# An identity made in DRAM, S5 input matrices loaded in rows and turned by TensorE, and small rows on other queues

## The chip, the cores and the metric

The kernel runs on one NeuronCore of a Trainium2 chip. A core has five engines that run their own instruction streams and meet through semaphores: TensorE (PE, with its weight loads as PEld), VectorE (DVE), ScalarE (ACT), GpSimd (POOL) and SyncE (SP). SP does no arithmetic here; it issues transfers. ACT and POOL issue a few transfers too, each on a queue of its own. The metric is the device time of one execution in microseconds (us), as the median of repeated runs.

## The reference

One layer of a diffusion backbone over 256 latent tokens, with 256 context tokens, all in float32, width 1024:

```python
mod = silu(c) @ w_mod + b_mod                  # shift, scale, gate; the same from c_ctx for the context
h   = rmsnorm(x, norm1_g) * (1 + sc1) + sh1    # and hc from ctx
proj = h @ w_in                                # columns: S5 input | K | V | Q | branch gates
# branch A: bidirectional S5, 32 groups of 16 channels, 64 complex states per group and direction
lbar = exp(lam * exp(log_step));  bbar = ((lbar - 1) / lam)[..., None] * (b_re + 1j * b_im)
#   diagonal scan over the context, its last state into the scan over the latents, readout with c, gelu, GLU
# branch B: grouped-query attention, normalised q and k, rotary positions
x_mix = x + g1 * (gates_a * (s @ w_ssm_out) + gates_b * (o @ w_attn_out)) @ w_out
# top 4 of 32 SwiGLU experts on the normalised x_mix: w_gate_up (1024 x 2048), w_down (1024 x 1024) each
out = rmsnorm(x_mix + g2 * experts, final_norm_g)
```

The S5 input matrices `s5_b_re` and `s5_b_im` have the shape direction x group x state x channel, 2 x 32 x 64 x 16 numbers each.

## The kernel before

On-chip memory is 24 pages of 128 partitions x 2048 numbers, and nearly everything lives in them. A transfer into a page may start only when the last reader of its earlier content is through. SP issues the large transfers strictly in program order (`load`, line 103). Behind the front part a list of 1 MB weight pieces (`stream`) is fed through pages as they come free (`release`): gates, GLU, output projections, and then per expert eight pieces of w_gate_up and four of w_down. The instructions of TensorE, VectorE and ScalarE come from a scheduler in the opening part, and from line 711 on mostly in the order in which they are written.

The opening part, to which all of the change belongs, goes so:

- SP loads x and ctx (four transfers of 512 KB), the small rows of the S5 eigenvalues (`lrows`, `lst`), then the modulation weights. `load_mod0(c, kk, page)` brings two 512 KB pieces of w_mod; c = 0 and c = 1 are two halves of the columns, four calls each. The two 1 MB pieces of the S5 input projection (`wu`) come between, and so do the four transfers of `s5_b_re` and `s5_b_im` into `b_raw` (lines 231 to 233). Those put the state index on the partitions, so that each run that is contiguous in DRAM is 16 numbers, 64 bytes.
- The identity matrix `ident`, by which TensorE transposes, is made on POOL by a fill and a masked select (`make_identity`, line 246; it shows as masks.py lines 197 and 199). The counting ramp `iot` (line 254) and the triangle `tri` are made there too.
- ScalarE and VectorE take the mean squares of x and ctx (`ss`); VectorE makes the reciprocal root from them (`rsqrt` into `rs`), by which both scale x and ctx in place.
- TensorE transposes the small rows `rows` into columns `cols`; from them come `sig` and the modulation input `scond`. It transposes `lrows` into `lam`, from which VectorE works out the S5 constants (`exp_acc` first).
- `h_raw` transposes x and ctx (32 transposes, copied out by ScalarE and VectorE into `hT`), while `mod0_mm(0, kk)` multiplies `scond` by the first half of the modulation weights. `mod0_copy`, `mod0_T` and `mod0_rows` turn the result into per-channel scale and shift, which are put on `hT`. Then `u_mm` (the S5 input projection) runs in turn with `mod0_mm(1, k)`.
- VectorE meanwhile makes `BB`, the scaled input matrices, from `b_raw`, and then, after `mod0_rows(1)`, the tables of `v_tables`.

Of the kernel before, what the change touches and what calls it, by code (L numbers as in the profile page):

```python
# [11 lines left out]
F32 = mybir.dt.float32  # L12
# [21 lines left out]
def hybrid_block(ctx: ExitStack, tc: tile.TileContext, a: dict, out: bass.AP):  # L34
    nc = tc.nc
# [20 lines left out]
    def w(name, *idx):  # L56
        return a[name][(0,) + idx] if idx else a[name][0]
# [16 lines left out]
    def sm(shape, name, dt=F32):  # L74
        return pool.tile(shape, dt, name=name)
# [27 lines left out]
    def load(dst, src):  # L103
        return tc.keep_in_program_order(SP.dma_start(dst, src))  # L104
# [11 lines left out]
    rows = sm([48, 128], "rows")  # L116
# [5 lines left out]
    load(lrows[0:32], w("s5_lam_re").rearrange("d g n -> g d n"))  # L122
    load(lrows[32:64], w("s5_lam_im").rearrange("d g n -> g d n"))
    load(lst[64:96], w("s5_log_step").rearrange("d g -> g d"))
    S.dma_start(rows[0:8], a["c"].rearrange("b (k p) -> (b k) p", p=128))
    S.dma_start(rows[8:16], a["c_ctx"].rearrange("(k p) -> k p", p=128))
    S.dma_start(rows[16:24], a["norm1_g"].rearrange("b (k p) -> (b k) p", p=128))
    G.dma_start(rows[28:44], w("b_mod")[0:2048].rearrange("(k p) -> k p", p=128))
    G.dma_start(rows[24:28], a["b_glu"].rearrange("b (k p) -> (b k) p", p=128))
# [97 lines left out]
    wu = [load_cols(w_in, 0, 512, 22, 0, 4)]  # L227
    for kk in range(4):
        load_mod0(1, kk, (18, 19, 20, 11)[kk])
        if kk == 0:  # L230
            for r, nm in ((0, "s5_b_re"), (1, "s5_b_im")):
                for d in range(2):
                    load(b_raw[64 * d:64 * d + 64, r], w(nm, d).rearrange("g n p -> n g p"))
        if kk == 2:
            wu.append(load_cols(w_in, 0, 512, 21, 4, 4))
# [9 lines left out]
    ident = sm([128, 128], "ident")  # L245
    make_identity(nc, ident)
# [97 lines left out]
    G.tensor_copy(lrows[64:96], lst[64:96].unsqueeze(2).to_broadcast([32, 2, 64]))  # L344
    ttrans(pl[:, 0:96], lrows.rearrange("p d n -> p (d n)"), ident[0:96, 0:96])
    lam = sm([128, 3, 32], "lam")
    with tc.issue_after(last.ins):
        V.tensor_copy(lam.rearrange("p r g -> p (r g)"), pl[:, 0:96])
# [203 lines left out]


# [1237 lines left out]
```

## Time and profile before

| | |
|---|---|
| runs, median (lowest to highest) | 1270.48 us (1269.86 to 1271.14) |
| the profiled execution | 1271.41 us |
| its span, first to last instruction | 1269.6 us |
| busy: PE / DVE / ACT / POOL | 1164.9 / 395.5 / 191.9 / 41.8 us |
| moved by the DMA engines | 462.54 MB, 364 GB/s over the span |
| DMA packets, and those under 512 B | 119134, 20669 |

The profile is of one execution. Its time is 1.8 us longer than its span; what lies around the span is launch and end. The span is read in stretches: an opening until about 92 us, the S5, attention and projection part until about 340 us, and the 32 experts after it.

### The profile page before, as it was taken

To read this page: it belongs to the slowest core of one execution; us is meant where nothing else is said; L and a number is where in the kernel's file an instruction comes from. 1 tells how busy PE (TensorE), PEld (TensorE's weight loads), DVE (VectorE), ACT (ScalarE), POOL (GpSimd) and SP (SyncE) were. 2 spreads that over 40 slices of the span, in tenths; PEclk is the share of its full clock that TensorE was granted. 3 is DMA by queue.
4 is the path that set the end of the run, shared out by engine and by line. 5 is a ranking of instruction groups with operands and counts; after the bars stand their busy time and mean duration, and the time that the engine had idled before them with its cause. 6 is when DMAs were issued, how large, how long until landed. Compare 5 with 4: busy or idle time off the path is not lost.

```text
span 1269.6 us, 16157 instructions
## 1 busy us (share of the span) xinstructions
PE 1164.9 (92%) x6759; PEld 532.9 (42%) x6760; DVE 395.5 (31%) x869; ACT 191.9 (15%) x358; POOL 41.8 (3%) x69
## 2 busy tenths in 40 slices
PE   3999996899899999999999898989898989999886
PEld 2775675798333333333323232323232323333224
DVE  4999963574211211111212111111111111111111
ACT  3241384542100000000000000000000000000002
POOL 1100140020000000000000000000000000000000
PEclk9999997999899999999999999999999999999999
DMA  9957484888899999999999999999999999999996
GB/s 283 303 194 263 139 194 98 278 317 333 331 412 417 416 417 417 416 417 417 417 417 417 418 416 418 417 418 416 417 418 417 417 416 417 417 416 417 416 392 196
DMA packets 119134, 462.54 MB, mean 364 GB/s; under 512 B 20669, under 2 KB 42345, under 8 KB 84242
## 3 DMA queue, kind: packets, MB, share of 16 engines
q1 hardware_dynamic: 117570, 458.31, 91.8%
q0 software_dynamic: 1440, 3.15, 1.4%
q8 instruction: 55, 0.90, 0.3%
q14 instruction: 21, 0.17, 0.0%
q10 hardware_dynamic: 48, 0.01, 0.0%
HBM read 459.89 MB, written 1.54 MB: 363 GB/s over the span
## 4 chain that ended last, share of the span: by engine, by line
PE 57%; DMA 32%; DVE 6%; issue 2%; ACT 2%; SPq 1%; POOL 0%; DVEq 0%; ACTq 0%; POOLq 0%
PE bk L97 54%; DMA pg<-in_w_gate_up_dram 28%; DVE pg L49 5%; PE bk L100 2%; DMA pg<-in_w_down_dram 2%; DMA pg<-in_b_gate_up_dram 2%; ACT pg L49 1%; SPq L104 1%; DMA pg<-in_w_in_dram 0%; DVE LS L49 0%; DVE smx L49 0%; ACT L49 0%; DVE rs_t L49 0%; DVE gate L49 0%; DVE gs__2634 L49 0%
## 5 line engine op out<-in xcount | busy, mean ns | idle before, releaser
L97 PE MATMUL bk<-pg,pg 128*64 128x512 f32 (+6 forms) x5424 | 998.7, 470 | 55.0 <-DMA pg<-in_w_down_dram 28.5
L97 PEld LDWEIGHTS bk<-pg,pg 128*64 128x64 f32 (+3 forms) x5424 | 445.0, 150 | 548.6 <-issue 360.4
L49 ACT ACTIVATE pg<-bk 128x512 f32<-128x512 f32 (+4 forms) x154 | 76.2, 521 | 745.1 <-PE bk L100 677.6
L49 DVE TENSOR_SCALAR pg<-bk 128x512 f32<-128x512 f32 x64 | 44.3, 692 | 294.3 <-PE bk L97 294.3
L49 DVE TENSOR_TENSOR pg<-pg,pg 128x1024 f32<-128x1024 f32 (+9 forms) x136 | 117.8, 891 | 25.6 <-ACT pg L49 24.4
L49 ACT ACTIVATE pg<-pg 128x512 f32<-128x512 f32 (+9 forms) x112 | 76.6, 697 | 246.9 <-DVE pg L49 214.9
L49 DVE TENSOR_TENSOR pg<-bk,shT 128x512 f32<-128x512 f32 x32 | 22.1, 692 | 270.5 <-PE bk L97 270.5
L49 DVE TENSOR_TENSOR pg<-bk,pg 128x512 f32<-128x512 f32 (+4 forms) x52 | 32.2, 619 | 221.2 <-PE bk L97 219.4
L100 PE MATMUL bk<-ident,pg 128*128 128x128 f32 x448 | 72.8, 290 | 10.6 <-DVE cmx L49 6.1
L100 PEld LDWEIGHTS bk<-ident,pg 128*128 128x128 f32 x448 | 50.6, 145 | 71.8 <-issue 42.0
L97 PE MATMUL bk<-pg 64*128 64x512 f32 (+1 forms) x368 | 70.3, 483 | 0.0
L97 PEld LDWEIGHTS bk<-pg 64*128 64x128 f32 (+1 forms) x368 | 19.8, 159 | 50.1 <-issue 50.1
L49 DVE TENSOR_TENSOR pg<-pg 128x512 f32<-128x512 f32 (+3 forms) x89 | 37.3, 434 | 3.6 <-ACT pg L49 3.0
L97 PE MATMUL bk<-pg,selB 128*64 128x512 bf16 (+1 forms) x196 | 34.3, 388 | 0.0
L49 DVE SCALAR_TENSOR_TENSOR pg<-pg 128x512 f32<-128x512 f32 (+3 forms) x67 | 30.3, 459 | 10.1 <-DMA pg<-in_x_dram 4.6
L1645 POOL DMA_DIRECT2D pg<-g2d x2 | 1.3, 640 | 887.3 <-PE bk L97 887.3
L97 PE MATMUL bk<-pg,scond 128*32 128x256 f32 (+1 forms) x256 | 26.9, 518 | 0.0
L49 DVE TENSOR_SCALAR pg<-iot,posp,gate 128x128 f32<-128x128 f32 x64 | 18.9, 340 | 0.0
L49 DVE TENSOR_TENSOR pg<-pg,LS 128x64 f32<-128x64 f32 (+4 forms) x36 | 15.9, 470 | 0.2
L97 PEld LDWEIGHTS <-selB 128*64 128x64 bf16 x196 | 9.0, 108 | 16.1 <-issue 15.9
L49 DVE TENSOR_SCALAR pg<-iot,posp,rs 128x64 f32<-128x64 f32 x64 | 15.7, 308 | 0.1
L49 DVE COPY pg<-bk 128x512 f32<-128x512 f32 (+1 forms) x24 | 14.5, 613 | 2.5 <-PE bk L100 2.5
(148 smaller groups left out, 180.1 us busy)
## 6 DMA issues: line engine op xcount, KB each, us to landing
pg<-in_w_gate_up_dram SPq DMA_DIRECT2D x256, 1024.0 KB, 19.9
pg<-in_w_down_dram SPq DMA_DIRECT2D x127, 1024.0 KB, 20.0
pg<-in_w_mod_dram SPq DMA_DIRECT2D x16, 1024.0 KB, 5.9
pg<-in_w_in_dram SPq DMA_DIRECT2D x13, 1024.0 KB, 5.7
pg<-in_w_mod_dram SPq DMA_DIRECT2D x16, 512.0 KB, 9.0
pg<-in_w_out_dram SPq DMA_DIRECT2D x4, 1024.0 KB, 8.4
pg<-Rd POOLq DMA_DIRECT2D x16, 128.0 KB, 8.0
pg<-in_w_ssm_out_dram SPq DMA_DIRECT2D x2, 1024.0 KB, 5.1
```

The costliest lines, as they stand in the source:

```text
L49: i = f(*ar, **kw)
L97: pinned(T.matmul(*ar, **kw))
L100: pinned(T.transpose(*ar))
L104: return tc.keep_in_program_order(SP.dma_start(dst, src))
L1645: G.dma_start(late["g2"][:, 512 * j:512 * j + 512], g2d[j:j + 1].to_broadcast([128, 512]))
```

## The change

The identity is no longer made on POOL. VectorE fills a strip `idz` of 128 x 129 numbers with zeros and its first column with ones; SP writes the strip to a DRAM tile `idd`, and reads the first 16384 numbers of it back as 128 rows of 128: a row pitch of 129 read with a pitch of 128 puts the ones on the diagonal. SP issues the write ahead of x and the read behind ctx.

`s5_b_re` and `s5_b_im` are loaded as they lie, with the group on 32 partitions and runs of 1024 numbers (4 KB), into page 6 (`b_rows`), ahead of the second half of the modulation weights. The new function `b_transposes` turns them by 16 transposes of 64 x 128, and ScalarE copies the results into `b_raw`. The second `wu` piece is loaded last of its group.

The rows of `c` and `c_ctx` keep ScalarE's queue; `lrows` and `lst` move there from SP's. `norm1_g` moves from ScalarE's queue to POOL's, and with `b_mod` and `b_glu` goes into a tile of its own, `rows2`, with a transpose of its own. The copy of `lst` into `lrows` moves from POOL to VectorE, and the copy into `lam` loses its order behind the scaling of x.

```diff
-    rows = sm([48, 128], "rows")
+    idz = pg(23, 0, 129)
+    V.memset(idz, 0.0)
+    V.memset(idz[:, 0:1], 1.0)
+    idd = dpool.tile([128, 129], F32, name="idd")
+    load(idd, idz)
+    ident = sm([128, 128], "ident")
+    rows = sm([16, 128], "rows")
+    rows2 = sm([28, 128], "rows2")
...
     for dst, nm in ((x_sb, "x"), (ctx_sb, "ctx")):
         for t in range(2):
             load(dst[:, t], a[nm][0, 128 * t:128 * t + 128])
-    load(lrows[0:32], w("s5_lam_re").rearrange("d g n -> g d n"))
-    load(lrows[32:64], w("s5_lam_im").rearrange("d g n -> g d n"))
-    load(lst[64:96], w("s5_log_step").rearrange("d g -> g d"))
+    load(ident, idd.rearrange("a b -> (a b)")[0:16384].rearrange("(p f) -> p f", f=128))
...
-    S.dma_start(rows[16:24], a["norm1_g"].rearrange("b (k p) -> (b k) p", p=128))
+    S.dma_start(lrows[0:32], w("s5_lam_re").rearrange("d g n -> g d n"))
+    S.dma_start(lrows[32:64], w("s5_lam_im").rearrange("d g n -> g d n"))
+    S.dma_start(lst[64:96], w("s5_log_step").rearrange("d g -> g d"))
+    G.dma_start(rows2[0:8], a["norm1_g"].rearrange("b (k p) -> (b k) p", p=128))
...
     wu = [load_cols(w_in, 0, 512, 22, 0, 4)]
+    b_rows = pg(6)
+    for r, nm in ((0, "s5_b_re"), (1, "s5_b_im")):
+        load(b_rows[32 * r:32 * r + 32].rearrange("p (d m) -> p d m", d=2), w(nm).rearrange("d g n p -> g d (n p)"))
     for kk in range(4):
         load_mod0(1, kk, (18, 19, 20, 11)[kk])
-        if kk == 0:
-            for r, nm in ((0, "s5_b_re"), (1, "s5_b_im")):
-                for d in range(2):
-                    load(b_raw[64 * d:64 * d + 64, r], w(nm, d).rearrange("g n p -> n g p"))
-        if kk == 2:
-            wu.append(load_cols(w_in, 0, 512, 21, 4, 4))
+    wu.append(load_cols(w_in, 0, 512, 21, 4, 4))
...
-    ident = sm([128, 128], "ident")
-    make_identity(nc, ident)
...
-    ttrans(pr[:, 0:44], rows[0:44], ident[0:44, 0:44])
+    ttrans(pr[:, 0:16], rows, ident[0:16, 0:16])
...
-    G.tensor_copy(lrows[64:96], lst[64:96].unsqueeze(2).to_broadcast([32, 2, 64]))
+    V.tensor_copy(lrows[64:96], lst[64:96].unsqueeze(2).to_broadcast([32, 2, 64]))
     ttrans(pl[:, 0:96], lrows.rearrange("p d n -> p (d n)"), ident[0:96, 0:96])
     lam = sm([128, 3, 32], "lam")
-    with tc.issue_after(last.ins):
-        V.tensor_copy(lam.rearrange("p r g -> p (r g)"), pl[:, 0:96])
+    V.tensor_copy(lam.rearrange("p r g -> p (r g)"), pl[:, 0:96])
+    pr2 = bank()
+    ttrans(pr2[:, 0:28], rows2, ident[0:28, 0:28])
+    V.tensor_copy(cols[:, 16:44], pr2[:, 0:28])
...
+    def b_transposes():
+        bv = b_rows[0:64].rearrange("p (n k) -> p k n", k=16)
+        for k8 in range(2):
+            b = bank()
+            for k in range(8):
+                ttrans(b[:, 64 * k:64 * k + 64], bv[:, 8 * k8 + k], ident[0:64, 0:64])
+            S.activation(b_raw[:, :, :, 8 * k8:8 * k8 + 8].rearrange("p r g k -> p (r g) k"),
+                         b.rearrange("p (k m) -> p m k", k=8), AF.Copy)
+
+    b_transposes()
```

SP's queue at its start, before; pg_60 and pg_61 hold x and ctx, pg_64 the S5 input matrices, pg_74 to pg_78 modulation weights, pg_82 the first `wu` piece, and DMAHW0 to DMAHW7 are the eight semaphores that transfers take in turn:

```order
L104 DMA pg_60<-in_x_dram 128x1024 x2
L104 DMA pg_61<-in_ctx_dram 128x1024 x2
L104 DMA lrows<-in_s_lam_re_dram 32x2x64
L104 DMA lrows<-in_s_lam_im_dram 32x2x64 [waits DMAHW0_49]
L104 DMA lst<-in_s_log_step_dram 32x2x1 [waits DMAHW1_49]
L104 DMA pg_74<-in_w_mod_dram 128x2x512 [waits DMAHW2_49]
...
L104 DMA pg_82<-in_w_in_dram 128x4x512 [waits DMAHW2_49]
L104 DMA pg_78<-in_w_mod_dram 128x2x512 [waits DMAHW3_49]
L104 DMA pg_78<-in_w_mod_dram 128x2x512 [waits DMAHW4_49]
L104 DMA pg_64<-in_s_b_re_dram 64x32x16 [waits DMAHW5_49]
L104 DMA pg_64<-in_s_b_re_dram 64x32x16 [waits DMAHW6_49]
```

The same place of SP's queue in the changed kernel; pg_83 is the strip of zeros and ones, pg_66 the new page of input matrices:

```order
L104 DMA idd<-pg_83 128x129 [waits DVE_49]
L104 DMA pg_60<-in_x_dram 128x1024 x2
L104 DMA pg_61<-in_ctx_dram 128x1024 [waits DMAHW0_49]
L104 DMA pg_61<-in_ctx_dram 128x1024 [waits DMAHW1_49]
L104 DMA ident<-idd 128x128 [waits DMAHW2_49]
L104 DMA pg_74<-in_w_mod_dram 128x2x512 [waits DMAHW3_49]
...
L104 DMA pg_82<-in_w_in_dram 128x4x512 [waits DMAHW3_49]
L104 DMA pg_66<-in_s_b_re_dram 32x2x1024 [waits DMAHW4_49]
L104 DMA pg_66<-in_s_b_im_dram 32x2x1024 [waits DMAHW5_49]
L104 DMA pg_78<-in_w_mod_dram 128x2x512 [waits DMAHW6_49]
L104 DMA pg_78<-in_w_mod_dram 128x2x512 [waits DMAHW7_49]
```

The write of the strip stands ahead of x and waits for VectorE, the read of the identity stands behind ctx and ahead of all weights, and the input matrices now stand ahead of pg_78.

TensorE's first instructions, before; pg_74 and pg_75 are modulation weights, pg_60 and pg_61 the scaled x and ctx:

```order
L100 MATMUL bk_153<-ident,rows 128x44
L100 MATMUL bk_183<-ident,lrows 128x96
L97 MATMUL bk_188<-pg_74,scond 32x256 x4
L100 MATMUL bk_246<-ident,pg_60 128x128 x4
L100 MATMUL bk_258<-ident,pg_60 128x128
L97 MATMUL bk_188<-pg_74,scond 32x256 x4
L100 MATMUL bk_240<-ident,pg_61 128x128 x4
...
L100 MATMUL bk_265<-ident,pg_69 128x128 x2
L100 MATMUL bk_288<-ident,pg_60 128x128 x4
L97 MATMUL bk_421<-pg_62,pg_82 128x256
```

The same two places of TensorE's stream in the changed kernel; pg_69 is the product that `mod0_T` transposes, and pg_62 with pg_82 is the start of `u_mm`:

```order
L100 MATMUL bk_153<-ident,rows 128x16
L100 MATMUL bk_182<-ident,lrows 128x96
L100 MATMUL bk_187<-ident,rows_90 128x28
L97 MATMUL bk_191<-pg_74,scond 32x256 x8
L100 MATMUL bk_249<-ident,pg_60 128x128 x4
L100 MATMUL bk_261<-ident,pg_60 128x128 x2
...
L100 MATMUL bk_268<-ident,pg_69 128x128 x2
L100 MATMUL bk_291<-ident,pg_60 128x128 x4
L100 MATMUL bk_418<-ident,pg_66 128x64 x8
L100 MATMUL bk_428<-ident,pg_66 128x64 x8
L97 MATMUL bk_444<-pg_62,pg_82 128x256
```

Both halves of the first modulation page now stand ahead of the transposes of x, and the sixteen transposes of the input matrices stand between `mod0_T(0)` and `u_mm`.

## Rows read from the trace of the kernel before

**Rows 1.** The page, its first line.

```profile
span 1269.6 us, 16157 instructions
```

**Rows 2.** Stretches: busy PE, PEld, DVE, ACT, POOL; granted clock, DMA share, GB/s.

```profile
0.00:10.00 10.00, 0.00 (x0) 0.01 (x1) 2.77 (x5) 4.66 (x8) 1.63 (x8) 1.00 0.77 260
10.00:20.00 10.00, 2.37 (x13) 1.16 (x14) 4.62 (x23) 2.11 (x4) 1.90 (x11) 1.00 1.04 388
...
400.00:600.00 200.00, 200.00 (x980) 73.61 (x980) 35.84 (x71) 11.66 (x22) 0.00 (x0) 1.00 1.02 417
```

**Rows 3.** Waits of SP's queue, 60 to 345 us: total, times, longest.

```profile
SPq L104 <- PE bk L97: 144.8, 32, 17.2
```

**Rows 4.** The chain that ended last, 0 to 60 us: start, length, what.

```profile
2.85 11.61 issue
...
14.71 0.27 POOL ident masks.py:199
...
32.71 16.78 PE bk L97 x120
...
50.95 9.41 DVE pg L49 x9
```

**Rows 5.** Timeline of the opening: start, length, engine, line, operation, idle before.

```profile
0.84 0.87 SPq L104 DMA_DIRECT2D pg<-in_x_dram  x2
0.96 0.27 DVE L49 MEMSET scond<- 128x256 f32 x1 [0.84 <-PEq L1775]
8.94 1.06 ACT L49 ACTIVATE pg<-pg 128x1024 f32<-128x1024 f32 x1
...
14.46 0.24 POOL L254 IOTA iot<- 128x128 f32 x1 [11.68 <-issue]
...
15.91 0.16 DVE L49 TENSOR_SCALAR rs_m<-ss 128x4 f32<-128x4 f32 x1
...
18.00 0.16 DVE L49 SCALAR_TENSOR_TENSOR rs<-rs_t,rs_y 128x4 f32<-128x4 f32 x1
...
19.40 1.33 PE L100 MATMUL bk<-ident,pg 128*128 128x128 f32 x5 [1.34 <-ACT pg L49]
...
26.36 0.29 DVE L49 TENSOR_TENSOR pg<-lam,pg 128x32 f32<-128x32 f32 x2
...
27.23 1.93 PE L97 MATMUL bk<-pg,scond 128*32 128x256 f32 x32
...
29.93 0.42 DVE L49 COPY pg<-bk 128x256 f32<-128x256 f32 x1
30.41 0.88 PE L100 MATMUL bk<-ident,pg 128*128 128x128 f32 x6 [1.24 <-DVE pg L49]
...
32.71 1.53 PE L97 MATMUL bk<-pg,pg 128*128 128x256 f32 x6 [1.43 <-ACT pg L49]
```

**Rows 6.** Busy time by stretch, two short stretches of the opening.

```profile
8.00:10.00 2.00, 0.00 (x0) 0.00 (x0) 0.36 (x1) 1.88 (x4) 0.00 (x0) 1.00 0.86 247
...
28.00:30.00 2.00, 1.16 (x24) 0.42 (x16) 1.73 (x11) 0.00 (x0) 0.00 (x0) 1.00 1.00 95
```

**Rows 7.** TensorE by form, 15 to 25 us: count, busy, mean of one.

```profile
L100 PE MATMUL bk<-ident,pg 128*128 128x128 f32 x16 | 4.0, 415 | 1.3 <-ACT pg L49 1.3
L97 PE MATMUL bk<-pg,scond 128*32 128x256 f32 x24 | 3.2, 635 | 0.0
```

**Rows 8.** The same, 25.8 to 50 us.

```profile
L97 PE MATMUL bk<-pg,scond 128*32 128x256 f32 x104 | 6.6, 384 | 0.0
L100 PE MATMUL bk<-ident,pg 128*128 128x128 f32 x16 | 2.5, 280 | 1.2 <-DVE pg L49 1.2
```

**Rows 9.** DMA issues of the whole run: size, and us to landing.

```profile
Rd<-pg POOLq DMA_DIRECT2D x8, 60.0 KB, 3.9
pg<-in_w_mod_dram SPq DMA_DIRECT2D x16, 512.0 KB, 9.0
```

**Rows 10.** Timeline, 126 to 153 us: sixteen transposes in a row.

```profile
141.61 2.00 PE L100 MATMUL bk<-ident,pg 128*128 128x128 f32 x16
```

More of the change, by code (lines that the diff above doesn't have):

```diff
@@ L121, in hybrid_block @@
             load(dst[:, t], a[nm][0, 128 * t:128 * t + 128])
-    load(lrows[0:32], w("s5_lam_re").rearrange("d g n -> g d n"))
-    load(lrows[32:64], w("s5_lam_im").rearrange("d g n -> g d n"))
-    load(lst[64:96], w("s5_log_step").rearrange("d g -> g d"))
+    load(ident, idd.rearrange("a b -> (a b)")[0:16384].rearrange("(p f) -> p f", f=128))
     S.dma_start(rows[0:8], a["c"].rearrange("b (k p) -> (b k) p", p=128))
     S.dma_start(rows[8:16], a["c_ctx"].rearrange("(k p) -> k p", p=128))
-    S.dma_start(rows[16:24], a["norm1_g"].rearrange("b (k p) -> (b k) p", p=128))
-    G.dma_start(rows[28:44], w("b_mod")[0:2048].rearrange("(k p) -> k p", p=128))
-    G.dma_start(rows[24:28], a["b_glu"].rearrange("b (k p) -> (b k) p", p=128))
+    S.dma_start(lrows[0:32], w("s5_lam_re").rearrange("d g n -> g d n"))
+    S.dma_start(lrows[32:64], w("s5_lam_im").rearrange("d g n -> g d n"))
+    S.dma_start(lst[64:96], w("s5_log_step").rearrange("d g -> g d"))
+    G.dma_start(rows2[0:8], a["norm1_g"].rearrange("b (k p) -> (b k) p", p=128))
+    G.dma_start(rows2[12:28], w("b_mod")[0:2048].rearrange("(k p) -> k p", p=128))
+    G.dma_start(rows2[8:12], a["b_glu"].rearrange("b (k p) -> (b k) p", p=128))
     b_raw = pg(4, 0, 1024).rearrange("p (r g k) -> p r g k", r=2, g=32)
@@ L316, in hybrid_block @@
     pr = bank()
-    ttrans(pr[:, 0:44], rows[0:44], ident[0:44, 0:44])
+    ttrans(pr[:, 0:16], rows, ident[0:16, 0:16])
     cols = sm([128, 48], "cols")
-    V.tensor_copy(cols[:, 0:44], pr[:, 0:44])
+    V.tensor_copy(cols[:, 0:16], pr[:, 0:16])
     n1c, bgl = cols[:, 16:24], cols[:, 24:28]
-    V.tensor_scalar(bgl, bgl, 0.5, None, op0=ALU.mult)
     bsh, bsc = cols[:, 28:36], cols[:, 36:44]
@@ L343, in hybrid_block @@
     pl = bank()
-    G.tensor_copy(lrows[64:96], lst[64:96].unsqueeze(2).to_broadcast([32, 2, 64]))
+    V.tensor_copy(lrows[64:96], lst[64:96].unsqueeze(2).to_broadcast([32, 2, 64]))
     ttrans(pl[:, 0:96], lrows.rearrange("p d n -> p (d n)"), ident[0:96, 0:96])
     lam = sm([128, 3, 32], "lam")
-    with tc.issue_after(last.ins):
-        V.tensor_copy(lam.rearrange("p r g -> p (r g)"), pl[:, 0:96])
+    V.tensor_copy(lam.rearrange("p r g -> p (r g)"), pl[:, 0:96])
+    pr2 = bank()
+    ttrans(pr2[:, 0:28], rows2, ident[0:28, 0:28])
+    V.tensor_copy(cols[:, 16:44], pr2[:, 0:28])
+    V.tensor_scalar(bgl, bgl, 0.5, None, op0=ALU.mult)
     lr, li, ls = lam[:, 0], lam[:, 1], lam[:, 2]
```

## The prediction

> **What bounds the kernel now.** I read the stretches first, from the back. From 400 us on the DMA engines move 417 GB/s without a break [rows 2]: the 32 experts are a stream of weights that is fed as pages come free, and the end comes when that stream is through. So the end moves with the moment at which the stream begins to flow without gaps, which the work ahead of it sets. There, by the waits of SP's queue, transfers wait for TensorE, 144.8 us in 32 waits between 60 and 345 us [rows 3], not TensorE for transfers. A gain in the opening is therefore handed on in full if it reaches the chain of engine work, and is lost if it only makes a transfer earlier.
>
> Then I read the chain of waits in the opening. It begins with 11.61 us in which POOL waits for nothing that the profile shows, and then comes the masked select that finishes the identity at 14.98 [rows 4]. The timeline says what stands there: the counting ramp at 14.46, with 11.68 us idle before it, ahead of the select in POOL's order [rows 5]. Everything that TensorE does needs the identity, and VectorE's order puts the sum `selS` of its columns ahead of the reciprocal root, so that `rs_m` runs at 15.91 though ScalarE's last square started at 8.94 [rows 5]. From 32.71 the chain is TensorE for 16.78 us, and from 50.95 VectorE's tables [rows 4]; both are plain work. The opening is late by what it waits for the identity.
>
> **The change part by part.** All sums are in the profiled execution's own time, 1271.41 us, of which 1269.6 is the span [rows 1]; it stands 0.93 above the median of 1270.48, and I take a shift of the one as a shift of the other.
>
> *When the new identity is there.* VectorE's first fill starts at 0.96 and takes 0.27 [rows 5]; the two new fills are no longer than that one, and the strip is ready at about 1.5. SP then issues the write (about 0.43, half of the 0.87 for two transfers of x [rows 5]), and x goes out at 1.95 instead of 0.84: +1.1. All transfers behind x move by this. How long a write to DRAM takes alone no row shows; the nearest is 3.9 us for 60 KB [rows 9], so SP can issue the read at 5.4. Its 64 KB stand behind ctx in SP's queue. ScalarE started on the last quarter of ctx at 8.94 [rows 5], so ctx lands by 10.05, and the identity at about 10.3 (64 KB at 388 GB/s [rows 2] are 0.2). Bounds: not below 10.05 as far as the root is concerned, since that needs ctx anyway; above, 5.4 + 9.0 = 14.4, if it takes as long as a weight piece issued into a full queue [rows 9]. I take 10.3, since it has only ctx ahead of it, not 3 MB of weights.
>
> *The root.* `rs_m` now waits for ScalarE's last square: 10.05 + 1.06 + 0.15 = 11.3, instead of 15.91: -4.6. The chain from `rs_m` to the end of `rs` took 18.16 - 15.91 = 2.25 for 11 dependent steps [rows 5], 0.2 each. The change puts steps of `exp_acc` between them, 24 instructions in all. Two that don't depend on each other take 0.29 together [rows 5], so that the second starts about 0.11 after the first. I take 24 x 0.115 = 2.8, or +0.5. The scaling of x starts 4.1 earlier. The `exp_acc` steps are thereby taken out of the stretch after it.
>
> *TensorE to the first modulation half.* One block of 8 records of 32x256 now runs ahead of the transposes of x, in the time in which TensorE waits for the scaling: 3.2 / 24 x 8 = 1.07 [rows 7], -1.0. The last block ended at 27.23 + 1.93 = 29.16, but VectorE's copy of the product started at 29.93 [rows 5], behind its `exp_acc` steps; these are now earlier: -0.7. Are the weights there? x, ctx and the first half of w_mod are 6.3 MB; 2.6 MB passed in the first 10 us and 3.88 in the next [rows 2], so they were through at 19.6, and will be at about 21, against a need at 23.5: yes. So far -5.8 at `mod0_rows(0)`.
>
> *The turning of the input matrices.* Sixteen transposes in a row took 2.00 us [rows 10]. The new ones are 64 wide instead of 128, which may make them as cheap as half of that, 1.0; their input is read with a stride of 64 bytes, which no row shows, and which could double it, 4.0. I take 2.0. They stand where TensorE waits 1.43 us for ScalarE's scaling of `hT` [rows 5], which covers that much: +0.6. They need their transfer: ahead of it in SP's queue stand 2.1 + 4.2 + 1.05 MB, with its own 0.52 MB 7.9 MB, which the engines passed at 20 + (7.9 - 6.48) / 0.388 = 23.7 before [rows 2]; with the 1.1 and the strip's two passages that is 25.1, and with up to 2 us until it is known to have landed, 25.1 to 27.1. TensorE comes there at 30.41 + 0.88 - 5.8 = 25.5. I take 26.2, a wait of 0.7. Together +1.3, with the bounds 0 and +4. ScalarE's two copies of 128x512 end long before VectorE needs `b_raw`.
>
> *What the old loads cost.* In 28 to 30 us, when they went through, the engines were fully busy with 95 GB/s [rows 6], and 0.52 MB take 5.5 us at that rate instead of 1.3 at 388 [rows 2]. Some 4 to 5 us of DMA time come free. I count them at nothing: in 32.7 to 50 TensorE runs without a wait for weights [rows 4], and after 60 us SP waits for TensorE [rows 3]. If that cover were gone they would be worth up to 4.2 us; that is a rival.
>
> *The small rows.* In 8 to 10 us the rate fell to 247 GB/s [rows 6] from the 388 around it [rows 2], while the small rows of SP's queue went through; were that dip gone, it would be worth 2 x 141 / 388 = 0.7. I count nothing, since the same rows pass through the same engines a little earlier. The Trainium skill, "DMA: Bandwidth & Descriptors", under "Issuing engines are not separate DMA queues", says so outright: another issuing engine saves only the time of issue. By that the sum stays as it is; if the page were wrong here it would be -5.2 instead of -4.5.
>
> *The sum.* -4.6 + 0.5 - 1.0 - 0.7 + 1.3 = -4.5 at the start of `u_mm`. From there the work is the same and in the same order, but for some VectorE steps of the scan that stand one place later; each takes about 0.7, either way. 1270.5 - 4.5 = 1266.0 us, and with the small unknowns together 1264.2 to 1267.9.
>
> **The rivals.**
>
> *Most of it is lost again on TensorE (within 0.2%).* The same forms take longer in 15 to 25 us than later: a transpose 4.0 / 16 = 0.25 against 2.5 / 16 = 0.156, a 32x256 record 0.133 against 0.063 [rows 7, 8], although the profile's column of the granted clock says 1.00 in both [rows 2, 6]. TensorE had worked on the transposes from 19.40 [rows 5] before it got faster, between the two stretches. If the rise doesn't come earlier with the work, because TensorE now starts before its weights and waits piece by piece, then what ran fast in 25.8 to 30 runs slow: 9 to 10 transposes and 40 records cost 0.9 + 2.8 = 3.7 more, and the time is 1269.7. The same time comes out if the input matrices land 3 us late. For it: TensorE's two first blocks come to their weights as these land. Against: from 15 us on it has 32 transposes to do without a break. In a sentence apart: the Trainium skill, "TensorE: Matmul & The Clock Gate", under "Part 1: The HAM clock gate", says that the array starts at the lower of its levels, 1.2 GHz, and that sustained work, not the moment, releases it to 2.4; by that rule the rise moves with the work and this rival fails, and the durations agree as far as they go.
>
> *The DMA time counts after all (faster by more).* If weights were late somewhere in the opening, hidden in long matmuls, the 4.2 us of 64-byte packets come on top: 1266.0 - 4.2 = 1261.8. Against it stand the waits of SP's queue [rows 3].
>
> *SP is held by the write (slower).* SP issues in order, and now all of the weights stand behind a read that waits for a write to DRAM. ctx keeps the engines in work until 10 us. If the write is confirmed late, first the identity and then every weight is late, at one us for each us. The gain of 4.5 is used up when the identity arrives at 14.8, and the kernel is slower by 0.2% from 17.3 on, for which the write would have to take some 15 us; with the identity at 18 the time is 1266.0 + 7.7 = 1273.7. The nearest row, 3.9 [rows 9], speaks against it.
>
> **How the numbers follow.** Forecast 0.58, lost on TensorE or late matrices 0.20, more by DMA 0.14, held by the write 0.08. About 0.2% (2.5 us) is what a measurement of this kernel can tell from no change. Faster is the forecast and the second rival, 0.72; same is 0.20; slower 0.08. The range takes the forecast's own, most of the first rival and a part of the DMA case: 1263.2 to 1269.2.
>
> **What would show it.** Right: the identity's first reader at 10 to 11 us, `rs_m` at about 11.4, the scaling of x at 14, `mod0_rows(0)` at about 25, `u_mm` at about 28.2, VectorE's tables from about 46.5, and the same shift at 400 us. Wrong: TensorE's transposes of the input matrices preceded by a wait of over 2 us; an idle SP between ctx and the weights; or a shift at 50 us that isn't there any more at 340 us.

## The result: slower, by 7 us

The changed kernel takes 1277.07 us (median of 8 runs, 1273.96 to 1280.20), the kernel before 1269.98 (8 runs, 1267.87 to 1271.17): a ratio of 1.0056 (95% interval 1.0042 to 1.0069). Forecast were 1266.0, with a range of 1263.2 to 1269.2. In the profiled executions it is 1280.2 against 1271.41, and the spans are 1278.4 and 1269.6 [rows 1]. The profiled execution of the changed kernel is the slowest of its eight, so the rows below show 8.8 us where the medians show 7.1.

The opening up to the first modulation half came much as forecast. The timeline of the changed kernel (start, length, engine, line, operation, idle before), to be laid beside [rows 5]:

```profile
1.42 0.34 SPq L104 DMA_DIRECT2D idd<-pg  x1
1.82 0.99 SPq L104 DMA_DIRECT2D pg<-in_x_dram  x2
...
3.80 0.65 SPq L104 DMA_DIRECT2D ident<-idd  x1
...
11.58 0.19 DVE L49 TENSOR_TENSOR selS<-ident 128x32 f32<-128x32 f32 x1 [0.28 <-DMA ident<-idd]
...
12.83 0.16 DVE L49 TENSOR_SCALAR rs_m<-ss 128x4 f32<-128x4 f32 x1
...
15.03 0.15 DVE L49 SCALAR_TENSOR_TENSOR rs<-rs_t,rs_y 128x4 f32<-128x4 f32 x1
...
25.34 0.42 DVE L49 COPY pg<-bk 128x256 f32<-128x256 f32 x1 [0.77 <-PE bk L97]
...
32.20 2.00 PE L100 MATMUL bk<-ident,pg 64*128 64x64 f32 x16 [5.50 <-DMA pg<-in_s_b_im_dram]
```

The copy of the product stands at 25.34 instead of 29.93: 4.6 us won. The last row is where it went. The 16 new transposes take 2.00 us, to the digit what was taken for them, but TensorE waits 5.50 us ahead of them. The issues of the same stretch (size, us from issue to landing) say for what:

```profile
pg<-in_s_b_im_dram SPq DMA_DIRECT2D x1, 256.0 KB, 16.1
```

Busy time by stretch in the changed kernel (columns as in [rows 2]; the last three are the granted clock, the DMA engines' busy share and GB/s):

```profile
0.00:10.00 10.00, 0.00 (x0) 0.01 (x1) 1.89 (x7) 2.69 (x5) 1.94 (x8) 1.00 0.69 219
22.00:23.00 1.00, 1.00 (x15) 0.61 (x13) 0.93 (x4) 0.71 (x2) 0.00 (x0) 1.00 1.05 387
24.00:26.00 2.00, 1.45 (x26) 0.70 (x19) 1.00 (x2) 0.00 (x0) 0.00 (x0) 1.00 1.08 136
26.00:28.00 2.00, 0.70 (x6) 0.46 (x5) 1.58 (x9) 1.24 (x3) 0.00 (x0) 1.00 1.03 169
28.00:30.00 2.00, 0.00 (x0) 0.00 (x0) 1.97 (x13) 0.84 (x2) 0.00 (x0) 1.00 1.01 261
31.00:37.00 6.00, 4.80 (x23) 4.17 (x24) 5.66 (x41) 1.19 (x2) 0.00 (x0) 0.50 1.05 385
150.00:154.00 4.00, 4.00 (x13) 3.24 (x12) 3.97 (x8) 0.60 (x1) 0.73 (x1) 0.57 0.00 0
400.00:600.00 200.00, 200.00 (x984) 73.92 (x982) 37.43 (x76) 11.88 (x22) 0.00 (x0) 1.00 1.02 417
```

From 24 to 28 us the engines are fully busy and move 136 and 169 GB/s, where they moved 387 at 22. That is the input matrices going through in 4 KB runs, above the 95 GB/s of the 64-byte runs in [rows 6] but at less than half of the 387. While TensorE waits it does nothing from 28 to 30, and then its granted clock is at 0.50, 1.2 instead of 2.4 GHz, from 31 to 37. The stream at the end moves 417 GB/s as before, so what is lost ahead of it is not made up there: 8.65 us at the router (below), 8.8 at the end of the span.

The chain of waits of the changed kernel shows two more losses on the way there:

```profile
15.94 16.12 DMA pg<-in_s_b_im_dram
32.20 2.00 PE bk L100 x16
34.20 18.54 PE bk L97 x120
...
95.22 42.34 PE bk L97 x264
137.57 5.74 DMA pg<-in_w_in_dram
...
150.15 5.16 PE bk L97 x16
155.33 6.75 DMA pg<-in_w_in_dram
...
187.40 21.40 DMA pg<-in_b_gate_up_dram
...
215.96 2.16 PE bk L97 x18
```

The same places in the kernel before:

```profile
92.00 42.34 PE bk L97 x264
134.35 5.08 DMA pg<-in_w_in_dram
...
180.03 20.03 DMA pg<-in_b_gate_up_dram
...
207.31 2.17 PE bk L97 x18
```

The first block of 120 matmuls takes 18.54 us at the fallen clock instead of 16.78 [rows 4]. So the 264 matmuls start 3.2 us later than before, not 4.5 earlier, and the router's first matmuls 8.65 later. Of these, 4.1 are added between the issue of the gate weights and that of the bias load, where the clock falls a second time (0.57 in 150 to 154; in the kernel before it was 1.00 there), and 1.4 in the landing of the bias load (21.40 against 20.03).

Over all runs the time goes with the clock. With c the mean granted clock of a run, 2 (1 - c) times its span is the time at the lower level: 42 us in the median of the changed kernel's 8 runs (c 0.981 to 0.985) against 33 in the runs of the kernel before (c 0.987). Among the 8 runs the time rises by 0.5 us for each us of it. At that rate the 9 us more would be worth 4.5 of the 7.1. This is a correlation and shows no cause, and c has three places, so a single value is good to some 1.3 us.

### The profile page after: what moved, and what is told of

It is laid out like the page before. It is cut to its first block, busy times and chain, and to the rows that moved or that the text cites. A ratio compares the mean times of both kernels' runs of the same rounds, so it can differ in the third digit from the quotient of the medians.

```text
span 1278.4 us, 16189 instructions
## 1 busy us (share of the span) xinstructions
PE 1171.1 (92%) x6776; PEld 537.3 (42%) x6777; DVE 394.8 (31%) x873; ACT 192.5 (15%) x360; POOL 43.4 (3%) x67
## 4 chain that ended last, share of the span: by engine, by line
DMA 49%; PE 42%; DVE 5%; ACT 2%; issue 1%; SPq 0%; DVEq 0%; ACTq 0%
PE bk L97 41%; DMA pg<-in_w_gate_up_dram 30%; DMA pg<-in_w_down_dram 14%; DVE pg L49 4%; PE bk L100 2%; DMA pg<-in_b_gate_up_dram 2%; ACT pg L49 2%; DMA pg<-in_s_b_im_dram 1%; DMA pg<-in_w_in_dram 1%; DMA pg<-in_w_mod_dram 1%; DMA pg<-in_x_dram 0%; SPq L104 0%; DVE LS L49 0%; DVE smx L49 0%; ACT L49 0%
## 5 line engine op out<-in xcount | busy, mean ns | idle before, releaser
L49 DVE TENSOR_TENSOR pg<-pg,pg 128x1024 f32<-128x1024 f32 (+8 forms) x136 | 117.5, 890 | 29.3 <-ACT pg L49 25.3
L100 PE MATMUL bk<-ident,pg 128*128 128x128 f32 (+1 forms) x464 | 74.7, 291 | 16.1 <-DVE cmx L49 6.1
L100 PEld LDWEIGHTS bk<-ident,pg 128*128 128x128 f32 (+1 forms) x464 | 52.5, 147 | 77.1 <-issue 47.7
L97 PE MATMUL bk<-pg,scond 128*32 128x256 f32 (+1 forms) x256 | 27.1, 518 | 0.7 <-DVE scond L49 0.7
```

What stands on the lines that cost most here:

```text
L49: i = f(*ar, **kw)
L97: pinned(T.matmul(*ar, **kw))
L100: pinned(T.transpose(*ar))
```

## The experiments

Ratios are to runs of the kernel before that were taken beside each kernel on the same chip; the medians come from several chips, so ratios are compared. The last three columns are from the one profiled execution, in us: the starts of the 264 matmuls (the end of the opening's effect) and of the router's first matmuls, and between them how long 48 matmuls near 145 us took. These take 4.19 at the full clock and 5.88 at the lower one. wide, far and wide_early compute other values and serve for the times alone.

| kernel | median us | ratio (95%) | us at half clock | 264 matmuls | 48 matmuls | router |
|---|---|---|---|---|---|---|
| before | 1269.98 | 1 | 33 | 92.00 | 4.19 | 207.31 |
| changed | 1277.07 | 1.0056 (1.0042 to 1.0069) | 42 | 95.22 | 5.88 | 215.96 |
| ident_only | 1271.35 | 0.9999 (0.9985 to 1.0014) | 30 | 93.22 | 4.19 | 209.50 |
| b_only | 1276.51 | 1.0037 (1.0023 to 1.0051) | 36 | 92.08 | 5.88 | 212.48 |
| wide | 1271.53 | 1.0000 (0.9988 to 1.0013) | 36 | 87.96 | 4.19 | 206.85 |
| late1 | 1275.86 | 1.0039 (1.0019 to 1.0060) | 38 | 89.69 | 4.19 | 206.90 |
| fill_open | 1271.90 | 1.0014 (0.9998 to 1.0031) | 33 | 92.25 | 4.19 | 210.13 |
| far (one run) | 1277.87 | | 41 | 93.98 | 5.88 | 213.94 |
| b_only_sooner | 1273.22 | 1.0017 (1.0003 to 1.0031) | 33 | 92.17 | 4.19 | 208.61 |
| after_sooner | 1273.15 | 1.0006 (0.9992 to 1.0020) | 38 | 88.70 | 5.88 | 209.67 |
| mid | 1273.11 | 1.0024 (1.0012 to 1.0037) | 38 | 89.03 | 5.65 | 209.79 |
| before_early | 1265.75 | 0.9958 (0.9944 to 0.9972) | 28 | 94.65 | 4.19 | 203.81 |
| after_early | 1271.25 | 0.9999 (0.9983 to 1.0016) | 33 | 94.36 | 4.19 | 205.28 |
| mid_early | 1266.01 | 0.9962 (0.9946 to 0.9978) | 28 | 89.10 | 5.82 | 199.73 |
| wide_early | 1263.63 | 0.9950 (0.9931 to 0.9969) | 25 | | 4.19 | 197.76 |
| before_early_fill | 1265.86 | 0.9949 (0.9930 to 0.9968) | 28 | 90.71 | 4.19 | 203.66 |
| mid_early_fill | 1269.65 | 0.9984 (0.9965 to 1.0004) | 30 | 89.51 | 4.19 | 205.01 |

A caution for reading it: before, before_early and before_early_fill have the same opening, and their 264 matmuls start at 92.00, 94.65 and 90.71. One profile places the opening within some 2 us only. In before_early it is the clock: TensorE waits 1.23 and 1.43 us ahead of `u_mm`, as in the kernel before, yet its clock is at 0.50 from 33 to 37 us, and the first 16 matmuls of `u_mm` take 6.70 us instead of 3.69. A long wait is not needed for a fall. Also, the profiled execution is the fastest of its kernel in late1, mid_early and wide_early, and the slowest in before_early. In wide_early the profile counts the 64 matmuls ahead of the 264 in with them, so its cell is empty.

### Which part of the change, and why the transfer is slow

**wide**: each matrix goes onto 128 partitions.

```diff
-        load(b_rows[32 * r:32 * r + 32].rearrange("p (d m) -> p d m", d=2), w(nm).rearrange("d g n p -> g d (n p)"))
+        load(b_rows[:, 512 * r:512 * r + 512], w(nm).rearrange("d g (h n) p -> (d g h) (n p)", h=2))
...
```

> The changed kernel with each input matrix loaded onto 128 partitions in 2 KB runs instead of 32 partitions in 4 KB runs; as many transposes of the same size, so the matrices' entries come out permuted. Theory A with few partitions as the cause of the slow transfer: it passes at over 300 GB/s, lands at 26 to 27.5 us, TensorE waits under 1.5 us, 1267 us (1266 to 1268.5). Rival C (the source is slow, 0.5 MB close together in DRAM, whatever the partitions): lands at 31 to 32 us, TensorE waits 5 us, 1273 to 1277 us.

**far**: the same 32 partitions, from rows far apart.

```diff
-        load(b_rows[32 * r:32 * r + 32].rearrange("p (d m) -> p d m", d=2), w(nm).rearrange("d g n p -> g d (n p)"))
+        load(b_rows[32 * r:32 * r + 32].rearrange("p (d m) -> p d m", d=2),
+             w_in[512 * r:512 * r + 512, 1280:2304].rearrange("(g d s) f -> g d s f", d=2, s=8)[:, :, 0])
```

> The changed kernel with the two loads reading 4 KB pieces of w_in that lie 106 KB apart, onto the same 32 partitions; the input matrices' values are others. Theory A (few partitions make the transfer slow): it lands at 31 to 33 us as in the changed kernel, at about 140 GB/s in 24 to 27 us. Rival C (0.5 MB close together in DRAM is what is slow): lands at 27 us.

The two stretches of the transfer, first in wide:

```profile
24.00:26.00 2.00, 1.45 (x25) 0.63 (x25) 1.12 (x2) 0.00 (x0) 0.00 (x0) 1.00 1.05 384
26.00:28.00 2.00, 1.68 (x18) 1.47 (x18) 1.47 (x8) 1.12 (x3) 0.00 (x0) 1.00 1.05 387
```

and in far:

```profile
24.00:26.00 2.00, 1.45 (x18) 0.77 (x10) 0.78 (x6) 0.00 (x0) 0.00 (x0) 1.00 1.03 146
26.00:28.00 2.00, 0.05 (x1) 0.00 (x0) 1.89 (x8) 1.89 (x4) 0.00 (x0) 1.00 1.03 186
```

How far apart the source rows lie doesn't matter, the number of partitions does: 384 against 136 and 146 GB/s for the same bytes. In wide the transposes start at 27.14 after a wait of 0.32 us, `u_mm` at 28.63, and the 264 matmuls 4.0 us earlier than before: close to the opening that was forecast. So A and against C on the transfer. The time is not A's 1267: at 1.0000 the 7 us of loss are gone, but the kernel is no faster than before. That is taken up below.

**ident_only**: the identity and the small rows as in the change, the input matrices as before.

```diff
-    for r, nm in ((0, "s5_b_re"), (1, "s5_b_im")):
-        load(b_rows[32 * r:32 * r + 32].rearrange("p (d m) -> p d m", d=2), w(nm).rearrange("d g n p -> g d (n p)"))
     for kk in range(4):
         load_mod0(1, kk, (18, 19, 20, 11)[kk])
+        if kk == 0:
+            for r, nm in ((0, "s5_b_re"), (1, "s5_b_im")):
+                for d in range(2):
+                    load(b_raw[64 * d:64 * d + 64, r], w(nm, d).rearrange("g n p -> n g p"))
...
-    b_transposes()
```

The second `wu` piece goes back to its old place too.

> Only the identity through DRAM and the small rows on other queues; the input matrices come as in the kernel before (64-byte runs, no transposes). Theory A (the input matrices' transfer is what costs): mod0_rows(0) at 26.3 as in the changed kernel, u_mm at 28.5, the clock stays at 1.00 to 60 us, VectorE's tables 4.2 us earlier than before, the same shift at 340 us: 1266 us (1265 to 1267). Rival B (the identity's way through DRAM or the later x is what costs): the scan stage from 140 us loses 4 us here too, 1270 us or more.

SP's queue in ident_only (start, length, issue):

```profile
16.83 12.25 SPq L104 DMA_DIRECT2D pg<-in_s_b_re_dram  x2
29.13 2.80 SPq L104 DMA_DIRECT2D pg<-in_s_b_im_dram  x2
31.97 3.07 SPq L104 DMA_DIRECT2D pg<-in_w_mod_dram  x4
```

and TensorE there (idle before, in brackets):

```profile
27.46 3.69 PE L97 MATMUL bk<-pg,pg 128*128 128x256 f32 x16 [1.43 <-DVE pg L49]
36.91 0.64 PE L97 MATMUL bk<-pg,scond 128*32 128x256 f32 x8 [1.11 <-DMA pg<-in_w_mod_dram]
38.38 0.64 PE L97 MATMUL bk<-pg,scond 128*32 128x256 f32 x8 [0.83 <-DMA pg<-in_w_mod_dram]
45.14 0.64 PE L97 MATMUL bk<-pg,scond 128*32 128x256 f32 x8 [1.47 <-DMA pg<-in_w_mod_dram]
46.51 0.86 PE L97 MATMUL bk<-pg,scond 128*32 128x256 f32 x8 [0.73 <-DMA pg<-in_w_mod_dram]
```

Neither theory foresaw this. TensorE starts `u_mm` at 27.46, 5.25 us earlier, and then waits 4.1 us in four pieces for the second modulation half, because SP is held over the two first 64-byte loads for 12.25 us and the weights stand behind them (issued from 31.97, in the kernel before from 29.47). Behind these waits the clock falls too: it is 0.60 from 47 to 51 us, and the last 8 matmuls of `u_mm` take 3.41 us instead of 1.99. So the old loads have a price in the opening once TensorE is early: the 264 matmuls start at 93.22, in wide at 87.96. In the whole time none of these 5.3 us is left, 0.9999 against 1.0000.

**b_only**: the kernel before with the change's lines on the input matrices alone (and the second `wu` piece last).

```diff
-            for r, nm in ((0, "s5_b_re"), (1, "s5_b_im")):
-                for d in range(2):
-                    load(b_raw[64 * d:64 * d + 64, r], w(nm, d).rearrange("g n p -> n g p"))
+    for r, nm in ((0, "s5_b_re"), (1, "s5_b_im")):
+        load(b_rows[32 * r:32 * r + 32].rearrange("p (d m) -> p d m", d=2), w(nm).rearrange("d g n p -> g d (n p)"))
...
+    b_transposes()
```

> Only the input matrices in 4 KB runs with the 16 transposes; identity and small rows as before. The identity is at 15 us, so TensorE reaches the transposes at about 31.3 us, when the transfer has just landed (31): a wait under 1 us, u_mm at 33.7, +1. VectorE's order in the scan stage is that of the changed kernel. Theory A1 (that order costs 4 us by itself): 1275 us. Theory A2 (only TensorE's wait of 5.5 us and the clock after it cost): 1271 us. Rival B: 1270 us, no loss without the identity's change.

1276.5 us: the time is near A1's, and A2 and B fall. TensorE has no wait for the matrices and the 264 matmuls start at 92.08, so the opening costs nothing; the loss comes between 144 and 210 us. TensorE in b_only there:

```profile
144.99 0.66 PE L100 MATMUL bk<-ident,pg 128*128 128x128 f32 x4 [1.31 <-DVE pg L49]
146.19 0.67 PE L100 MATMUL bk<-ident,pg 128*128 128x128 f32 x4 [0.54 <-DVE pg L49]
146.69 5.88 PE L97 MATMUL bk<-pg,pg 128*128 128x256 f32 x48
```

and in **b_only_sooner**, which has these transposes in one piece (its edit below is against b_only):

```profile
145.71 1.25 PE L100 MATMUL bk<-ident,pg 128*128 128x128 f32 x8 [1.76 <-DVE pg L49]
146.80 4.19 PE L97 MATMUL bk<-pg,pg 128*128 128x256 f32 x48
```

```diff
+    for r, nm in ((0, "s5_b_re"), (1, "s5_b_im")):
+        load(b_rows[32 * r:32 * r + 32].rearrange("p (d m) -> p d m", d=2), w(nm).rearrange("d g n p -> g d (n p)"))
     wu = [load_cols(w_in, 0, 512, 22, 0, 4)]
-    for r, nm in ((0, "s5_b_re"), (1, "s5_b_im")):
-        load(b_rows[32 * r:32 * r + 32].rearrange("p (d m) -> p d m", d=2), w(nm).rearrange("d g n p -> g d (n p)"))
```

> The kernel with only the input matrices changed, their two loads one place sooner in SP's queue (ahead of the 1 MB piece of w_in instead of behind it). TensorE waits for them in neither kernel; what changes is VectorE's order in the scan stage, which is that of the kernel before here. Theory A1 (that order, which lets TensorE idle a little longer at 144 us so that its clock falls, is what the change costs): TensorE's wait at 144 us is 1.1 in one piece as before, granted clock 1.00 there, 1271 us (1270 to 1273). Rival H (the 4 KB runs or the transposes cost it, whatever the order): 1275 to 1277 us as in that kernel.

In b_only the granted clock is 0.59 from 146 to 150, the 48 matmuls take 5.88 us instead of 4.19, and the page that they free is refilled later. With VectorE's order of before, 1.0037 becomes 1.0017, but the intervals overlap, and in b_only_sooner the clock falls one wait later (0.57 from 154 to 158).

**after_sooner**: the same move in the changed kernel.

> The changed kernel with the same move of the two loads. The order of VectorE in the scan stage is that of the kernel before. The matrices land about 2.5 us sooner, TensorE waits 3 us instead of 5.5. Theory A1: opening 0 to +1 against before, no loss in the scan stage: 1271 to 1273 us. Rival H: 1275 us or more.

Here the matrices land at 26.9 and TensorE waits 0.37 us; the 264 matmuls start 3.3 us earlier than before, and the time is 1.0006. The transfer onto 32 partitions is still there, so in this kernel too most of the 7 us are gone with TensorE's wait for it. A1's mechanism fails here, however. These are the transposes and the 48 matmuls first in after_sooner, which has the order of before in one piece and loses its clock, and then in fill_open (below), which has the changed order in two pieces and keeps it:

```profile
142.01 1.32 PE L100 MATMUL bk<-ident,pg 128*128 128x128 f32 x8 [1.71 <-DVE pg L49]
143.17 5.88 PE L97 MATMUL bk<-pg,pg 128*128 128x256 f32 x48
```

```profile
145.06 0.66 PE L100 MATMUL bk<-ident,pg 128*128 128x128 f32 x4 [1.21 <-DVE pg L49]
146.35 0.63 PE L100 MATMUL bk<-ident,pg 128*128 128x128 f32 x4 [0.64 <-DVE pg L49]
146.82 4.19 PE L97 MATMUL bk<-pg,pg 128*128 128x256 f32 x48
```

The order does not decide whether the clock falls, then, and that it costs anything by itself is not shown. What the profiles agree on is the clock. From the start of the 264 matmuls to the router, the five kernels with the old bias loads whose 48 matmuls ran slow (changed, b_only, far, after_sooner, mid) take 120.0 to 121.0 us, and the six others 115.3 to 118.9. What makes the clock fall in one kernel and not in another stays open.

### What TensorE's wait costs through its clock

**fill_open**: TensorE is given work while it waits.

```diff
+    bf_ = bank()
+    for i in range(34):
+        ttrans(bf_[:, 128 * (i % 4):128 * (i % 4) + 128], pg(9, 1024, 128), ident)
     b_transposes()
```

> The changed kernel with 34 transposes of 128x128 of data that is there, into a scratch bank, ahead of the 16 transposes, so that TensorE works through most of its wait for the input matrices. Theory K (the wait makes the granted clock fall to half from 31 to 38 us, and that costs 1.8 us of its own): the clock stays at 1.00 there, the block of 120 takes 16.8 instead of 18.5 us, the scan stage as in the changed kernel, 1274 to 1275.5 us. Rival: the clock falls all the same or the 16 transposes come later; 1277 us.

TensorE in fill_open, and the stretch that was at 0.50:

```profile
26.52 6.49 PE L100 MATMUL bk<-ident,pg 128*128 128x128 f32 x56 [0.55 <-DVE pg L49]
```

```profile
31.00:37.00 6.00, 6.00 (x41) 5.08 (x44) 5.69 (x47) 1.19 (x2) 0.00 (x0) 1.00 1.05 388
```

The clock stays at 1.00, and with 34 useless transposes the kernel is 5 us faster (1.0014 instead of 1.0056). That is K's direction, but its size was too small: the time at half clock falls from 42 to 33 us, that is by more than the 6 us of this one place. In the two profiles, 1.8 us are the block of 120 and 1.2 an earlier start of `u_mm` (32.94 against 34.13, the matrices having landed at 29.2 instead of 32.1); the rest comes behind 140 us, where the clock did not fall a second time.

**late1**: the transposes and the VectorE steps that need them (`b_bar` holds the six lines on `BB`) moved behind the second eighth of `u_mm`.

```diff
-    b_transposes()
...
     for k in range(3):
         for q in range(4):
             u_mm(q, k)
         mod0_mm(1, k)
+        if k == 1:
+            b_transposes()
+            b_bar()
...
```

> The changed kernel with the 16 transposes and the six VectorE steps that need them moved behind the second eighth of u_mm and of the second modulation half. The slow transfer stays. Theory A (TensorE's wait is what the transfer costs): the transposes stand at about 37 us without a wait, u_mm at 28.5, 1266 to 1267.5 us. Rival D (the transfer's hold on the engines costs by itself, since the weights of the second half stand behind it): TensorE waits 3 us or more for them at 31 us, 1270 us or more.

In its profile `u_mm` starts at 28.00, and TensorE waits 0.28 for the next weights, not 3 us; the opening is 2.3 us earlier than before. A's time fails: 1275.86 (1270.91 to 1276.96) and not 1266 to 1267.5. D's time, 1270 or more, came, but not the wait that was to cause it. The profiled execution is the fastest of the six, so what the others lost can't be seen. A loss of some 5 us without TensorE's wait, as in b_only, is left without a cause.

### Where an earlier opening goes

**mid**: late1 with the matrices' loads behind the second piece of the second half.

```diff
     for kk in range(4):
         load_mod0(1, kk, (18, 19, 20, 11)[kk])
+        if kk == 1:
+            for r, nm in ((0, "s5_b_re"), (1, "s5_b_im")):
+                load(b_rows[32 * r:32 * r + 32].rearrange("p (d m) -> p d m", d=2),
+                     w(nm).rearrange("d g n p -> g d (n p)"))
...
```

> The changed kernel with the input matrices' loads behind the second of the four weight pieces of the second modulation half, and the 16 transposes with their VectorE steps behind the second eighth of u_mm. Theory A (the slow transfer costs only where TensorE waits for it or for what stands behind it): no wait over 0.7 us in the opening, u_mm at 28.3, the last scan tables and the 264 matmuls 4.2 us earlier than before (87.8 instead of 92.0). With theory E most of it is gone at 207 us: 1269 to 1271 us. Rival G (nothing swallows it): 1266 us.

A's opening came, for the most part: TensorE waits for no transfer, `u_mm` starts at 27.86 and the 264 matmuls at 89.03, 3.0 us earlier than before. The time, 1273.11 (1.0024), is above both forecasts. In its profile the clock is at 0.50 from 144 to 146 us, after a wait of 1.75 us for VectorE, and the router starts 2.5 us later than before.

**before_early**, **after_early**, **mid_early**: the first three narrow loads of bias rows are issued four steps earlier, in the kernel before, the changed kernel and mid (at 160.57 us in before_early, at 178.95 before).

```diff
-            for _ in range(3):
+            for _ in range(3 if n else 4):
                 yield
...
+        if u == 5:
+            next(bias_left)
         if u == P_M:
```

> The kernel before with one edit elsewhere: the first three narrow bias loads (pg<-in_b_gate_up, 32 partitions each, 20 us to landing) are issued four steps earlier, at about 165 instead of 179 us; ScalarE uses them at the same place. Theory E (a gain of the opening is swallowed at 190 to 200 us, where ScalarE's in-order queue and so the shift logits, the softmax and TensorE wait for this load, whose landing the DMA engines set): the wait of 10.6 us goes, TensorE is at the router's 16 matmuls at 198 to 200 instead of 207.3 us: 1262 us (1260 to 1265). Rival F (POOL's 16 gathers of 128 KB land no earlier and hold the same place, or something in the weights does): 1268 to 1271 us.

> The changed kernel with the same move of the bias loads. Theory E: the losses of the opening (3.2) and of the scan stage (4.1) are before that place and stay, the wait goes: 1262 + 7 = 1269 us, about 8 less than the changed kernel. Rival F: 1275 to 1278 us.

> The one before with the bias loads issued four steps earlier as well. Theory E: with the place gone that swallows gains, the opening's 4 us come through: 1262 - 4 = 1258 us (1256 to 1261), 4 less than the kernel before with early bias loads. Rival F or G: 1266 us or more.

The place in the kernel before, by stretch and by ScalarE's waits from 180 to 210 us (total, times, longest):

```profile
180.00:190.00 10.00, 8.69 (x65) 6.81 (x64) 5.31 (x10) 9.34 (x16) 3.37 (x6) 1.00 1.07 173
190.00:200.00 10.00, 4.63 (x38) 4.25 (x36) 0.00 (x0) 0.00 (x0) 0.00 (x0) 0.95 1.08 153
```

```profile
ACT pg L49 <- DMA pg<-in_b_gate_up_dram: 10.6, 1, 10.6
```

The same wait list of before_early:

```profile
ACT pg L49 <- DMA pg<-in_w_in_dram: 5.2, 1, 5.2
```

The place is real: in the kernel before, ScalarE and VectorE stand still from 190 to 200 us for a load onto 32 partitions, with the DMA engines full at 153 GB/s (POOL's gathers run there too). Moving that load brings some 5 us in the kernel before (0.9958) and 6 to 7 in the changed one. E had forecast 8 in each and the router at 198 to 200 us; it starts at 203.81, since another transfer, `w_in`, is then waited for at the same place, 5.2 us. And E's second half fell: mid_early, forecast at 1258, is no faster than before_early, although its opening is earlier. It too waits for `w_in`, 3.1 us, and its clock fell near 145 us.

**wide_early**, and two with transposes of the identity into a scratch bank (`fill(n)` does n of them) where TensorE waits at 141 us; the edit of mid_early_fill:

```diff
         for h4 in range(2):
+            if t and h4:
+                fill(13)
             b = bank()
```

> The changed kernel with the input matrices on 128 partitions (entries permuted) and the bias loads issued four steps earlier. Theory E (only the place at 200 us swallows the opening's 4 us): 4 less than the kernel before with early bias loads, ratio to the kernel before 0.993, 1261 to 1263 us. Theory M (the 2.9 us of gain were gone in the same way in the two kernels with early bias loads: the stretch from 140 to 200 us takes the rest back): ratio 0.996, 1265 to 1267 us.

> The kernel with later input matrices and early bias loads, with 13 transposes of the identity into a scratch bank where TensorE waits 1.76 us at 141 us. Theory L (what takes the gain back in 140 to 200 us is TensorE's clock, which falls after that wait): granted clock 1.00 from 140 to 155 us, 3 us less than without the transposes, ratio to the kernel before 0.993 to 0.994. Theory M2 (it is the order of VectorE and the transfers there, not the clock): ratio 0.996 as without.

> The kernel before with early bias loads and 9 such transposes at the same place, where it waits 1.07 us and its clock did not fall: the control. Both theories: within 1 us of the kernel without them, ratio 0.995 to 0.997.

wide_early, at 0.9950, lies between the two theories and within the intervals of before_early (0.9958) and before_early_fill (0.9949): that anything of its earlier opening comes through is not shown. mid_early_fill tells nothing on L: its 13 transposes themselves waited 1.76 us for VectorE, it seems for their scratch bank, and so filled nothing; the clock fell all the same (0.50 from 144 to 146), and the kernel got no faster (0.9984 against 0.9962, with intervals that overlap). The 9 of before_early_fill waited 1.28. What takes the opening's gain back between 140 and 210 us stays open. Where the 48 matmuls ran slow, the clock goes with it. In wide they did not, and there only the places can be seen, against the kernel before: 4.0 us ahead when the gate weights are issued (130.31 against 134.35), 1.9 when the bias load is issued (178.11 against 180.03), 0.5 at the router, the bias load having taken 21.57 instead of 20.03 us to land.

Of the kernels that compute the same, before_early is among the fastest, 1265.75 us, and it holds nothing of the change; mid_early, which holds the change with its matrices moved, is as fast.

## Why the prediction was wrong, point by point

- *When the new identity is there*: taken 10.3, measured 11.58. The write to DRAM was no obstacle (the read is issued at 3.80, where 5.4 was taken). x cost more: it landed at 7.0 instead of 4.5, and the first 10 us moved 219 GB/s instead of 260 [rows 2].
- *The root*: -4.6 forecast, -3.1 measured (12.83 against 15.91), for the same reason. The interleaved steps cost 0.1, not 0.5. The earlier block and the copy brought what was forecast. At the first modulation half: -4.6 instead of -5.8. This part of the mechanism was right, with sizes off by 1.2.
- **The step that failed** is the turning of the input matrices, "I take 26.2, a wait of 0.7. Together +1.3, with the bounds 0 and +4." The transposes were right (2.00), the landing was wrong: 32.1, a wait of 5.50, because I passed the 0.52 MB at the 388 GB/s of full transfers [rows 2]. From -4.6 at the copy it goes to +1.4 at `u_mm` (34.13 against 32.71), so this step cost 6.0, beyond its own bound. wide and far show why: 32 partitions at a time. At full rate, in wide, the transposes could start at 27.14, the upper end of the 25.1 to 27.1 that I gave, and the kernel is at 1.0000 instead of 1.0056: with this step mended the 7 us of loss are gone. It is not the only way to lose them: late1, mid and b_only have no such wait and are still 3 to 5 us behind the kernel before. The trace of before had a row that should have warned me, the stretch with narrow loads at 153 GB/s, and my sum passed it over. The Trainium skill says it too: "SBUF — State Buffer", under "Door 1: The DMA port swizzle", has partitions 0 to 31, and 0 to 63 as well, reach 8 of the 16 ports, so half the rate. Direction and trace agree; measured was 136 of 384 GB/s, about a third.
- The wait had a second price that the sum didn't hold, the clock: 1.8 us in the block of 120. With it the opening adds up: -4.6 + 6.0 + 1.8 = +3.2 at the 264 matmuls. My first rival had matrices 3 us late at 1269.7; they were 6 late, and it did not count the clock after the wait. Its other half did not come: the records of 32x256 get short from 20.91 on in the changed kernel, from 25.96 on before, so the faster forms moved with the work.
- *"From there the work is the same"* failed too, and it is why the 4.5 us of gain would not have come through. Even with the late transfer mended, in wide, a start 4.0 us earlier at the 264 matmuls is 0.5 at the router and nothing in the time. I had read that ahead of 345 us transfers wait for TensorE [rows 3], and the chain of waits only to 60 us [rows 4]; further on, the chain of the kernel before has TensorE's chain waiting for transfers, 5.08 and 20.03 us (shown above). In the changed kernel, b_only, after_sooner and mid a second fall of the clock stands in the same stretch; VectorE's order there, which I priced at ±0.7, does not decide it. b_only loses 5 us there. Why the clock falls, and what takes the gain in wide, stays open.
- *What the old loads cost*: counted at nothing, with TensorE running without a wait for weights as the cover. ident_only shows that this cover was thinner than the 5 us by which TensorE came earlier. My second rival priced it at 4.2; TensorE's four waits are 4.1. Its sign was right in the opening, if the new transfer is fast, as in wide; in the time nothing of it is seen.
- *Held by the write*: this rival did not come, since the read was issued at 3.80.

## What to carry to other kernels

Price a transfer by the partitions that it lands on and not by its run length alone, and look in the trace for another narrow load before taking the full rate. A wait that the change puts ahead of TensorE can cost more than its length: in the three profiles with a wait of 4.9 to 5.5 us here (changed, after_early, far) the lower clock came behind it, and work of no use in that wait was the cheaper choice. A gain in an early stage is worth what is left of it at the next place where in-order engines wait for a transfer that doesn't move with it, so follow the shift through every such place before carrying it 1:1.

## What the runs showed of the hardware

- While 0.52 MB in 4 KB runs went onto 32 partitions a load, the DMA engines moved 136 to 169 GB/s, and 384 with the same bytes in 2 KB runs onto 128, with the engines' busy share over 1 in both. The eight weight pieces issued around them, from 14 to 34 us, took 15.3 us to land (median) against 11.0 in wide.
- TensorE's granted clock fell to 0.50 after a wait of 5.5 us in the opening of the changed kernel. It also fell to 0.50 in before_early after waits of 1.23 and 1.43, where the kernel before, with the same instructions and waits, kept 1.00. After waits of 1.71 to 1.76 us near 142 us it fell in after_sooner, mid and mid_early, and it did not in wide, and in b_only_sooner only after the next wait: the length of one wait doesn't decide it. The 8 runs of the changed kernel lie 6 us apart, in step with it.
- SP was held 12.25 us over two loads of 64-byte runs in ident_only, and all weights behind it.
